# Two groups of FFN tiles ahead of the first down projection, and one more group with the gate in block products

## The chip, the cores and the metric

The kernel runs on one core of one Trainium2 chip. The metric is device time in microseconds (us) of one execution; the time before is the median of three runs, 1040.7 us (1040.25 to 1043.4).

## The reference

Two decoder layers on a sequence of 512 tokens with 1024 channels, in float32. Each layer is a normalized mixer with a residual, then a normalized gated FFN with a residual; at the end comes one more normalization. The FFN is what the change touches:

```
g  = hn @ w_gate                   # 1024 -> 2816
g  = causal_dwconv3(g, conv_w) + conv_b
up = hn @ w_up                     # 1024 -> 2816
h  = h + (silu(g) * up) @ w_down   # 2816 -> 1024
```

## The kernel before

**Number format.** Every matrix product is done in three matmuls of a rounded 32-bit type (`mm3`, lines 132 to 135): each operand is split into a rounded high part and the remainder (`hi`, `lo`), and `hi*hi`, `hi*lo` and `lo*hi` are added in one PSUM bank. The splits cost work on the other engines: ScalarE (ACT) makes `hi`, VectorE (DVE) subtracts it from the original to get `lo` (`parts`, L128 and L129; `split`, L247 and L249). In `summed` (L120 to L122) ACT writes the negative of `hi` into `lo`, and an accumulating DMA issued by GpSimd (POOL) adds the original.

**Buffers.** Original weights land in `raw` (4 buffers, loaded by the queue of SyncE, SP); their halves lie in `whi` and `wlo` (6 each). PSUM has seven banks for products (`mm`) and one for small work (`aux`).

**The FFN.** Its 2816 channels are 22 tiles of 128, taken two at a time: a group is named by its first tile, f = 0, 2, ... 20. `hidden(f)` computes the two activation tiles of a group, `a_f` and `a_f+1`, in one of four ways:
- f = 0, `direct` with `normed` false: the input is `h` times its gain, not yet divided by its norm; the norm is applied when the products leave PSUM. In the same call stand `pair_weights(2, ...)`, which loads and splits the weights of group 2, and `normalize` (L566 on), four times, which rewrites the eight pairs `hg` with the normalized input and builds the sums `t23`, `t41` that the block products need. Only then comes `rest()`, which takes group 0 out of PSUM (L555, conv at L504 and L506, silu at L512, the product with POOL at L558, the product with `up` at L561, then the split into `a_hi`, `a_lo`).
- f = 2, `direct` with `normed` true: 96 matmuls of 128x512, first the two gate tiles (48), then the two up tiles.
- f = 6, 10, 14, 18, `both`: gate and up each as a 2x2 block product (two tiles of output channels, two halves of the input channels, two halves of the tokens) in seven products instead of eight, in the manner of Strassen. Each product is 12 matmuls of 128x256. The stationary sides are sums and differences of weight blocks (`s12`, `s34`, L652 to L659), which DVE builds and then splits.
- the others (4, 8, 12, 16, 20), `seven`: the up tiles as such a block product (84 matmuls of 128x256), the gate tiles directly (48 of 128x512).

**The order of the work.** `PARTS` (L474) cuts the tiles into parts. For each part the groups of that part are computed in turn, and then the part's tiles are multiplied with their rows of `w_down` and added: to `h` in layer 0 (`project`, L292), to `y`, tokens in partitions, in layer 1 (`group8`, add at L1009). The parts are (0, 2), (2, 6), (6, 10), (10, 14), (14, 18), (18, 22): the first down projection uses two tiles (48 matmuls of 128x512), the others four (96). In layer 0 the last part also transposes the parameters of layer 1 (`params`, L92). A scheduler orders the instructions at build time by priorities close to the program's order and its own estimates; each engine then runs its list strictly in order. Activation tiles `a` have four buffers for each half, block sums (`sum`) three, the rows that the convolution reads three.

Of the kernel before, what the change touches and what calls it, by code (L numbers as in the profile page):

```python
# [30 lines left out]
def tile_trunk(ctx: ExitStack, tc: tile.TileContext, x, norm_mix, norm_ffn, final_norm,  # L31
# [13 lines left out]
    def mm_bank(name):  # L45
        return ps_mm.tile([P, 512], F32, tag="mm", name=name)
# [22 lines left out]
    def params1():  # L69
        return params("1", [  # L70
            ("mix", rows_of(norm_mix[1]), NK), ("bsp", b_spatial[0], NK),
            ("ffn", rows_of(norm_ffn[1]), NK), ("cf", conv_rows(conv_ffn[1]), 3 * NF),
            ("bf", rows_of(b_conv_ffn[1]), NF)])
# [39 lines left out]
    def weights(src, a, b, name):  # L113
        return parts(*fetch(src, a, b, name))
# [108 lines left out]
    def newton(ms, n, name, r):  # L223


        sd = work("sd", n, name)
        nc.scalar.activation(sd, ms, AF.Sqrt)
        nc.vector.reciprocal(r, sd)
        nc.vector.tensor_tensor(ms, ms, r, ALU.mult)
        nc.vector.scalar_tensor_tensor(ms, ms, -0.5, r, op0=ALU.mult, op1=ALU.mult)  # L230
# [42 lines left out]
    def project(name, w, acts, ks, norm, before=None):  # L273

        for gi in range(2):
            c0 = gi * 512
            chunks = {}
            for i in range(0, len(ks), 2):
                k0 = min(ks[i], ks[i + 1])
                hi, lo = weights(  # L280
                    w[k0 * P : (k0 + 2) * P, c0 : c0 + 512].rearrange("(k p) c -> p k c", p=P),
                    2, 512, f"{name}_{gi}_{k0}")
                chunks[k0], chunks[k0 + 1] = (hi, lo, 0), (hi, lo, 1)

            def lhs(k, j):
                hi, lo, n = chunks[k]
                cs = slice(j * P, (j + 1) * P)
                return hi[:, n, cs], lo[:, n, cs]

            def done(j, ps):  # L290
                k = gi * 4 + j
                nc.vector.tensor_tensor(h[k], ps, h[k], ALU.add)  # L292
                if norm is not None:
                    norm.add(k)

            group(f"{name}{gi}", range(4), ks, lhs, lambda k, j: acts[k], 4, done,
                  before if gi == 0 else None)
# [173 lines left out]
            return nxt  # L471


    PARTS = ((0, 2), (2, 6), (6, 10), (10, 14), (14, 18), (18, 22))  # L474
    HALF = S // 2
    BOTH = (6, 10, 14, 18)
    NP = NK // 2
    PAIRS = [k for i in range(NP) for k in (i, i + NP)]

# [7 lines left out]
    class Ffn:  # L487
# [307 lines left out]
        def hidden(self, f, before=lambda i, j: None):  # L795
            if f == 0:
                def first(i, j):
                    before(i, j)
                    if (i, j) == (1, 0):
                        self.norm.rstd_tokens()  # L800
                    elif (i, j) == (2, 2):
                        self.r = self.norm.rstd_spread()

                ch = self.pair_weights(0, [("g", 0), ("u", 0), ("g", 1), ("u", 1)])
                rest = self.direct(0, False, (range(4),), ch, first)
                self.ch = self.pair_weights(2, [("g", 0), ("g", 1), ("u", 0), ("u", 1)], "g")
                for kp in range(NP):
                    self.normalize(kp)
                rest()
            elif f == 2:  # L810
                self.direct(2, True, ((0, 1), (2, 3)), self.ch)()
            elif f in BOTH:
                self.both(f)
            else:
                self.seven(f)

    def ffn0(norm):
        nonlocal prm1
        with tc.tile_pool(name="f0", bufs=1) as ap:
            def sums(kp):  # L820
                return [ap.tile([P, 2, HALF], F32R, name=f"t23{i}_{kp}") for i in "hl"]

            ffn = Ffn(0, prm0, norm, ap, sums)
            nxt = None
            for a, b in PARTS:
                for f in range(a, b, 2):
                    ffn.hidden(f)
                if b == NF:
                    prm1 = params1()
                    nxt = Norm("m1", lambda k: prm1("mix", k))  # L830
                project(f"d0_{a}", w_ffn_down[0], ffn.acts, list(range(a, b)), nxt)
            return nxt
# [126 lines left out]
    def ffn1(norm):  # L959
        with tc.tile_pool(name="f1", bufs=1) as ap:  # L960
            def sums(kp):
                return [cp.tile([P, 2, HALF], F32R, tag=f"h{k}", name=f"t23_{k}")
                        for k in (kp, kp + NP)]

            ffn = Ffn(1, prm1, norm, ap, sums)
            acts = ffn.acts
            y = [ap.tile([P, D], F32, name=f"y{t}") for t in range(NT)]
            ssf = ap.tile([P, NT, PAD], F32, name="ssf")[:, :, :2]

            def turn_residual(t, half):  # L970
                ps = mm_bank(f"hT{t}_{half}")
                for i in range(4):
                    nc.tensor.transpose(ps[:, i * P : (i + 1) * P],
                                        h[half * 4 + i][:, t * P : (t + 1) * P], ident)
                nc.scalar.copy(y[t][:, half * 512 : (half + 1) * 512], ps)

            def before(i, j):
                if i < 2:
                    turn_residual(j, i)

            for a, b in PARTS:
                for f in range(a, b, 2):
                    ffn.hidden(f, before=before)
                last = b == NF
                if last:
                    fin = wp.tile([P, D], F32, tag="raw", bufs=4, name="fin")
                    nc.scalar.dma_start(
                        fin, final_norm.rearrange("(o d) -> o d", o=1).to_broadcast([P, D]))
                    root = small[:, 2:3]
                    nc.scalar.activation(root, eps, AF.Sqrt)  # L990
                ch = {}
                for ft in range(a, b):
                    ch[ft] = weights(w_ffn_down[1][ft * P : (ft + 1) * P, :]
                                     .rearrange("(k p) c -> p k c", p=P), 1, D, f"dn1_{ft}")

                def lhs(ft, j):
                    ts_ = slice((j // 2) * P, (j // 2 + 1) * P)
                    return acts[ft][0][:, ts_], acts[ft][1][:, ts_]

                def rhs(ft, j):  # L1000
                    c = slice((j % 2) * 512, (j % 2 + 1) * 512)
                    return ch[ft][0][:, 0, c], ch[ft][1][:, 0, c]

                yf = {}

                def done(j, ps):
                    t, half = j // 2, j % 2
                    dst = y[t][:, half * 512 : (half + 1) * 512]
                    nc.vector.tensor_tensor(dst, ps, dst, ALU.add)  # L1009
                    if not last:  # L1010
                        return
                    sq = tp.tile([P, S], F32, tag="sq", name=f"sqf{j}")
                    ss = ssf[:, t, half : half + 1]
                    nc.scalar.activation(sq, dst, AF.Square, accum_out=ss)
                    yf[half] = ap.tile([P, S], F32, tag="s", bufs=3, name=f"yf{j}")
                    nc.vector.tensor_tensor(yf[half], dst, fin[:, half * 512 : (half + 1) * 512],
                                            ALU.mult)
                    if half == 0:
                        nc.vector.tensor_scalar(ss, ss, 1.0 / D, EPS, op0=ALU.mult, op1=ALU.add)
                        return  # L1020
                    ms = ssf[:, t, 0:1]
                    nc.vector.scalar_tensor_tensor(ms, ss, 1.0 / D, ms, op0=ALU.mult, op1=ALU.add)
                    r = tp.tile([P, LINE], F32, tag="rc", name=f"rc_fin{t}")[:, :1]
                    newton(ms, 1, f"fin{t}", r)
                    nc.vector.tensor_scalar(ms, ms, 1.5, None, op0=ALU.add)
                    for c in range(2):
                        cs = slice(c * 512, (c + 1) * 512)
                        nc.vector.tensor_scalar(y[t][:, cs], yf[c], r, ms,
                                                op0=ALU.mult, op1=ALU.mult)
                        nc.sync.dma_start(out[t * P : (t + 1) * P, cs], y[t][:, cs])  # L1030

                group8(f"dn{a}", list(range(a, b)), lhs, rhs, 4, done)
# [12 lines left out]

    n = mixer0()
    n = ffn0(n)
    n = mixer1(n)
    ffn1(n)


# [28 lines left out]
```

## Time and profile before

| | |
|---|---|
| runs (3) | 1040.25, 1040.7, 1043.4 us; median 1040.7 |
| profiled execution | 1041.7 us, its span 1040.0 us |
| mean granted clock of TensorE | 0.983 |
| DVE busy | 660.4 us, 64% of the span |
| HBM read, written | 98.42 MB, 2.10 MB |

In the profile PE is TensorE's matmuls and PEld its weight loads, which run beside them. A row of the timeline gives start and duration in us, the engine, the line, the operation, the tiles (output <- inputs), and in brackets how long the engine had been idle and what released it. A row of the waits gives the engine and what it wanted, what it waited for, the total in us, the count and the longest. `d` are the banks of the down projection in layer 0, `dn` in layer 1, `gu` those of groups 0 and 2, `u_4a` and the like those of a block product of group 4. A matmul's duration contains the filling and draining of the array, so successive matmuls overlap, and the pace is read from starts.

### The profile page before, as it was taken

To read this page: it belongs to the slowest core of one execution; us is meant where nothing else is said; L and a number is where in the kernel's file an instruction comes from. 1 tells how busy PE (TensorE), PEld (TensorE's weight loads), DVE (VectorE), ACT (ScalarE), POOL (GpSimd) and SP (SyncE) were. 2 spreads that over 40 slices of the span, in tenths; PEclk is the share of its full clock that TensorE was granted. 3 is DMA by queue.
4 is the path that set the end of the run, shared out by engine and by line. 5 is a ranking of instruction groups with operands and counts; after the bars stand their busy time and mean duration, and the time that the engine had idled before them with its cause. 6 is when DMAs were issued, how large, how long until landed. Compare 5 with 4: busy or idle time off the path is not lost.

```text
span 1040.0 us, 13829 instructions
## 1 busy us (share of the span) xinstructions
PE 999.5 (96%) x5475; PEld 865.6 (83%) x5475; DVE 660.4 (64%) x977; ACT 495.0 (48%) x725; POOL 91.9 (9%) x107
## 2 busy tenths in 40 slices
PE   8999996899999999999999999949999999999997
PEld 6888885688988989899888888837889899898985
DVE  5976539638576586756833545495477756767576
ACT  6423447235453536436655434662426436353463
POOL 3041121100000000000300001220000000000000
PEclk9999998799999999999999999979999999999999
DMA  7432244324354453554343223451335544354432
GB/s 234 166 102 81 83 120 110 94 77 123 104 142 112 133 138 106 142 135 124 119 130 101 81 86 97 101 117 45 89 94 142 142 124 141 82 142 142 123 82 81
DMA packets 80462, 119.25 MB, mean 115 GB/s; under 512 B 4133, under 2 KB 53517, under 8 KB 80397
## 3 DMA queue, kind: packets, MB, share of 16 engines
q1 hardware_dynamic: 73580, 98.96, 30.2%
q0 software_dynamic: 5472, 17.83, 9.7%
q10 hardware_dynamic: 1344, 1.58, 0.5%
q8 instruction: 43, 0.70, 0.3%
q14 instruction: 23, 0.18, 0.1%
HBM read 98.42 MB, written 2.10 MB: 97 GB/s over the span
## 4 chain that ended last, share of the span: by engine, by line
PE 91%; DVE 3%; issue 3%; DMA 2%; ACT 0%; SPq 0%; POOL 0%; DVEq 0%; POOLq 0%; ACTq 0%
PE d L133 4%; PE d L134 4%; PE dn L135 4%; PE dn L133 4%; PE dn L134 4%; PE d L135 4%; PE g L133 4%; PE g L134 4%; PE g L135 3%; PE gu L133 2%; PE gu L135 2%; PE gu L134 2%; PE v L133 1%; PE oo L135 1%; PE u L134 1%
## 5 line engine op out<-in xcount | busy, mean ns | idle before, releaser
L133 PE MATMUL dn<-whi_dn,a_hi 128*128 128x512 f32 x176 | 69.3, 395 | 14.9 <-ACT a_hi L247 14.9
L133 PE MATMUL d<-a_hi,whi_d 128*128 128x512 f32 x176 | 68.1, 398 | 14.6 <-ACT a_hi L247 14.6
L134 PE MATMUL d<-a_lo,whi_d 128*128 128x512 f32 x176 | 69.4, 396 | 0.0
L134 PE MATMUL dn<-wlo_dn,a_hi 128*128 128x512 f32 x176 | 68.9, 393 | 0.0
L135 PE MATMUL d<-a_hi,wlo_d 128*128 128x512 f32 x176 | 68.9, 392 | 0.0
L135 PE MATMUL dn<-whi_dn,a_lo 128*128 128x512 f32 x176 | 68.5, 394 | 0.0
L506 DVE SCALAR_TENSOR_TENSOR c<-rows,prm,c 128x512 f32<-128x512 f32 x88 | 66.5, 770 | 0.4
L133 PE MATMUL g<-hgh,whi_g 128*128 128x512 f32 x160 | 62.5, 391 | 0.0
L134 PE MATMUL g<-hgl,whi_g 128*128 128x512 f32 x160 | 62.5, 391 | 0.0
L135 PE MATMUL g<-hgh,wlo_g 128*128 128x512 f32 x160 | 62.2, 389 | 0.0
L1009 DVE TENSOR_TENSOR y<-dn,y 128x512 f32<-128x512 f32 x48 | 32.8, 690 | 37.1 <-PE dn L135 37.0
L133 PEld LDWEIGHTS dn<-whi_dn,a_hi 128*128 128x128 f32 x176 | 33.4, 190 | 22.7 <-ACT a_hi L247 16.0
L133 PEld LDWEIGHTS d<-a_hi,whi_d 128*128 128x128 f32 x176 | 33.3, 191 | 22.6 <-ACT a_hi L247 15.9
L129 DVE TENSOR_TENSOR wlo_dn<-raw_dn,whi_dn 128x1024 fp32r<-128x1024 f32 x22 | 26.8, 1224 | 35.4 <-ACT whi_dn L128 35.4
L129 DVE TENSOR_TENSOR wlo_d<-raw_d,whi_d 128x1024 fp32r<-128x1024 f32 x22 | 26.8, 1224 | 35.4 <-ACT whi_d L128 35.4
L129 DVE TENSOR_TENSOR wlo_g<-raw_g,whi_g 128x1024 fp32r<-128x1024 f32 x24 | 29.3, 1222 | 30.4 <-ACT whi_g L128 26.6
L292 DVE TENSOR_TENSOR h<-d,h 128x512 f32<-128x512 f32 x48 | 32.7, 689 | 20.1 <-PE d L135 19.5
L247 ACT ACTIVATE a_hi<-s 128x512 fp32r<-128x512 f32 x44 | 27.4, 628 | 34.3 <-DVE s L792 13.3
L121 POOL DMA_DIRECT2D wlo_u<-raw_u x18 | 15.4, 858 | 306.6 <-ACT wlo_u L120 175.6
L129 DVE TENSOR_TENSOR wlo_u<-raw_u,whi_u 128x1024 fp32r<-128x1024 f32 x16 | 19.6, 1224 | 34.2 <-ACT whi_u L128 34.1
L135 PEld LDWEIGHTS dn<-whi_dn,a_lo 128*128 128x128 f32 x176 | 33.3, 189 | 8.5 <-DVE a_lo L249 1.3
L134 PEld LDWEIGHTS d<-a_lo,whi_d 128*128 128x128 f32 x176 | 33.6, 191 | 7.9 <-DVE a_lo L249 0.7
(911 smaller groups left out, 3135.7 us busy)
## 6 DMA issues: line engine op xcount, KB each, us to landing
raw_u<-in_w_ffn_up_dram SPq DMA_DIRECT2D x36, 512.0 KB, 3.8
raw_g<-in_w_ffn_gate_dram SPq DMA_DIRECT2D x36, 512.0 KB, 4.5
raw_d<-in_w_ffn_down_dram SPq DMA_DIRECT2D x22, 512.0 KB, 3.6
raw_dn<-in_w_ffn_down_dram SPq DMA_DIRECT2D x22, 512.0 KB, 3.7
wlo_u<-raw_u POOLq DMA_DIRECT2D x18, 512.0 KB, 5.2
wlo_g<-raw_g POOLq DMA_DIRECT2D x12, 512.0 KB, 5.1
raw_oe<-in_w_out_even_dram SPq DMA_DIRECT2D x8, 512.0 KB, 3.5
raw_g<-in_w_ffn_gate_dram SPq DMA_DIRECT2D x16, 256.0 KB, 2.8
```

The source lines that it names most:

```text
L121: nc.gpsimd.dma_start(lo, raw, accum_op=ALU.add)
L129: nc.vector.tensor_tensor(lo, raw, hi.bitcast(F32), ALU.subtract)
L133: nc.tensor.matmul(ps, lhs[0], rhs[0], start=start, stop=False)
L134: nc.tensor.matmul(ps, lhs[0], rhs[1], start=False, stop=False)
L135: nc.tensor.matmul(ps, lhs[1], rhs[0], start=False, stop=stop)
L247: nc.scalar.activation(hi, src, AF.Copy, scale=scale)
L292: nc.vector.tensor_tensor(h[k], ps, h[k], ALU.add)
L506: nc.vector.scalar_tensor_tensor(c, t[:, i : S + i], prm("cf", i * NF + ft), c, op0=ALU.mult, op1=ALU.add)
L1009: nc.vector.tensor_tensor(dst, ps, dst, ALU.add)
```

## The change

Two edits in the FFN, both for both layers. The list of parts now names the groups to be computed ahead of each projection: groups 0 and 2 come before the projection of tiles 0 and 1, and group 4 alone before that of tiles 2 to 5. And group 4 goes from `seven` to `both`, so that five of the nine block groups have the gate in block products too.

```
-    PARTS = ((0, 2), (2, 6), (6, 10), (10, 14), (14, 18), (18, 22))
+
+    PARTS = (((0, 2), 0, 2), ((4,), 2, 6), ((6, 8), 6, 10), ((10, 12), 10, 14),
+             ((14, 16), 14, 18), ((18, 20), 18, 22))
     HALF = S // 2
-    BOTH = (6, 10, 14, 18)
...
-            elif f in BOTH:
+            elif f % 4 == 2 or f == 4:
                 self.both(f)
...
-            for a, b in PARTS:
-                for f in range(a, b, 2):
+            for groups, a, b in PARTS:
+                for f in groups:
                     ffn.hidden(f)
...
-            for a, b in PARTS:
-                for f in range(a, b, 2):
+            for groups, a, b in PARTS:
+                for f in groups:
                     ffn.hidden(f, before=before)
```

In the order that the scheduler builds, PE's list has the 96 matmuls of group 2 ahead of the 48 of the small projection in both layers, 168 matmuls of 128x256 for group 4 in place of 84 and 48, and the parameter transposition of layer 0 behind group 20 instead of behind group 0. POOL has one accumulating DMA more per layer. SP issues the same loads; only the four of group 4 change places among themselves. All lines of the kernel after L474 move down by one.

## Prediction

> **What bounds the kernel now.** I read the page's busy shares first, then what TensorE (PE) waited for, then its timeline around the longest waits.
>
> ```profile
> PE 999.5 (96%) x5475; PEld 865.6 (83%) x5475; DVE 660.4 (64%) x977; ACT 495.0 (48%) x725; POOL 91.9 (9%) x107
> PE   8999996899999999999999999949999999999997
> PEclk9999998799999999999999999979999999999999
> ```
>
> PE carries the span, with two dips (slices 7 and 8, and 27; the clock falls in the same slices). The waits say what they are:
>
> ```profile
> PE dn L133 <- ACT a_hi L247: 14.9, 2, 14.3
> PE d L133 <- ACT a_hi L247: 14.6, 2, 14.2
> ```
>
> In each layer PE waits once for some 14 us at the first matmul of the small down projection, for `a_hi`, the activations of FFN tile 0. PE's timeline, layer 0 and then layer 1:
>
> ```profile
> 172.02 0.40 PE L135 MATMUL gu<-hgh,wlo_u 128*128 128x512 f32 x1
> 172.25 0.26 PE L92 MATMUL prm_ps<-ident,pk 112*128 112x112 f32 x1
> 186.71 1.22 PE L133 MATMUL d<-a_hi,whi_d 128*128 128x512 f32 x2 [14.20 <-ACT a_hi L247]
> ...
> 201.10 0.39 PE L133 MATMUL gu<-hgh,whi_g 128*128 128x512 f32 x1
> ...
> 222.86 0.28 PE L623 MATMUL u_4a<-hgh,whi_a 128*128 128x256 f32 x1
> ...
> 243.86 0.40 PE L133 MATMUL d<-a_hi,whi_d 128*128 128x512 f32 x1
> ...
> 265.68 0.28 PE L623 MATMUL g_6a<-hgh,whi_a 128*128 128x256 f32 x1
> ...
> 285.83 0.28 PE L623 MATMUL u_8a<-hgh,whi_a 128*128 128x256 f32 x1
> ...
> 686.70 0.39 PE L135 MATMUL gu<-hgh,wlo_u 128*128 128x512 f32 x1
> 701.38 0.80 PE L133 MATMUL dn<-whi_dn,a_hi 128*128 128x512 f32 x1 [14.30 <-ACT a_hi L247]
> ...
> 715.23 0.39 PE L133 MATMUL gu<-hgh,whi_g 128*128 128x512 f32 x1
> ...
> 736.99 0.28 PE L623 MATMUL u_4a<-hgh,whi_a 128*128 128x256 f32 x1
> ...
> 757.98 0.40 PE L133 MATMUL dn<-whi_dn,a_hi 128*128 128x512 f32 x1
> ```
>
> So in layer 0: group 0 ends at 172.25, the small projection runs from 186.71, group 2 from 201.10, group 4 from 222.86, the next projection from 243.86. Durations overlap on PE, so all prices below are differences of starts. The stretches around the wait also show the clock:
>
> ```profile
> 180.00:190.00 10.00, 3.29 (x7) 1.99 (x7) 10.00 (x12) 4.78 (x7) 4.67 (x4) 0.50 0.67 157
> 190.00:192.00 2.00, 1.56 (x4) 0.96 (x4) 1.52 (x4) 0.63 (x1) 0.00 (x0) 0.50 0.00 0
> 192.00:203.00 11.00, 11.00 (x49) 9.06 (x48) 6.82 (x10) 1.69 (x2) 0.00 (x0) 0.97 0.15 48
> ```
>
> (Columns: sum, PE, weight loads, DVE, ACT, POOL busy; then granted clock, DMA.) When PE comes back at 186.71 its clock is 0.50 and stays there until about 192. The hole thus costs its 14 us and a slow start behind it. DVE is full from 180 to 190: it normalizes `h`, and evacuates group 0 in the same queue.
>
> **The change, part by part.**
>
> *1. Group 2 ahead of the small projection.* It does not wait for `a_0`, only for the normalized `hg`. Its 96 matmuls took 222.86 - 201.10 = 21.76 us, 0.227 each. The 48 of the projection cost 48 x 0.227 = 10.88 at that pace; they took 201.10 - 186.71 = 14.39 in layer 0 and 13.85 in layer 1, the rest being the slow clock and a second wait of about 0.5. New start of group 2: 172.25. Is its input there? PE needs the pairs of `hg` in order, each pair of k feeding 12 matmuls (2.72 us) of the first set: at 172.25, 174.97, 177.7 and 180.4. The last halves come from DVE:
>
> ```profile
> 176.36 0.69 DVE L555 TENSOR_TENSOR rows<-gu,rstd_f 128x512 f32<-128x512 f32 x1
> 176.96 1.30 DVE L576 TENSOR_TENSOR hgl<-x,hgh 128x512 fp32r<-128x512 f32 x2
> ...
> 185.32 0.68 DVE L561 TENSOR_TENSOR s<-gu,s 128x512 f32<-128x512 f32 x1
> ...
> 190.84 0.68 DVE L249 TENSOR_TENSOR a_lo<-s,a_hi 128x512 fp32r<-128x512 f32 x1
> ...
> 691.63 1.29 DVE L576 TENSOR_TENSOR hgl<-x,hgh 128x512 fp32r<-128x512 f32 x2
> ```
>
> They are done at 178.26 (layer 1: 692.92, wanted at 686.93 + 8.16 = 695.1), about 2 us early. Weights of group 2 were loaded and split before in both orders (SP's list keeps its order here, but for group 4's four loads). Banks: group 0 holds four of seven until DVE reads them; the first set of group 2 takes two, the second the seventh and the one that `rows<-gu` has read at 177.05. No wait, price 0.
>
> *2. What follows on ACT and DVE.* Before, ACT waited for DVE ahead of each `a_hi`:
>
> ```profile
> 186.03 0.63 ACT L247 ACTIVATE a_hi<-s 128x512 fp32r<-128x512 f32 x1 [2.57 <-DVE s L561]
> ...
> 190.17 0.63 ACT L247 ACTIVATE a_hi<-s 128x512 fp32r<-128x512 f32 x1 [2.76 <-DVE s L561]
> ```
>
> ```profile
> L504 ACT ACTIVATE c<-rows,prm 128x512 f32<-128x512 f32 x44 | 31.7, 720 | 0.4
> ```
>
> In the built order ACT now has, ahead of `a_0_hi`, the two `whi_a` of group 4, two copies `rows<-gu_2` and one tap `c_2`; ahead of `a_1_hi` also `c_3` and `s_2`. Copies wait for PE's first set, done at 172.25 + 10.88 = 183.13, when ACT comes to them at about the same time, so nobody behind them (`a_0_hi`, whose input comes at 185.3 + 0.68) is held. On DVE three taps of group 2 and two `wlo_a` come ahead of `a_1_lo`, in place of four sums of group 4 and a parameter copy. ACT: seven instructions of at most 0.72 (a tap, the dearest of them), 5.0 us more, against 2.57 + 2.76 = 5.3 that it waited there. Between the product at 185.32 and `a_1_lo` DVE has three taps and a `wlo_a` (3 x 0.77 + 0.69 = 3.0) for three sums and the copy (3 x 0.69 + 0.26 = 2.3), 0.7 more; I allow 0.5 for the two `whi_a`, which ACT has ahead of `s_0`. So `a_1_lo` ends at 191.52 + 1.2 = 192.7. PE wants it when it has done group 2 and three matmuls: 172.25 + 21.76 + 0.68 = 194.7. Margin 2 us; without it each us late costs one, plus the slow clock once the wait is as long as above.
>
> *3. Group 4 in block products for gate and up.* It takes away 84 matmuls of 128x256 with 48 of 128x512 (243.86 - 222.86 = 21.00) and puts 168 of 128x256, as group 6 has them: 285.83 - 265.68 = 20.15. Gain 0.85. Its price lies elsewhere: seven stationary sets instead of six, and only 10.88 us of projection before it starts, instead of 10.88 + 21.76. I put the work in DVE's queue from `a_1_lo` on:
>
> ```profile
> L652 DVE TENSOR_TENSOR s12g<-raw_g,raw_g x8: 684/688/694, 246.9 to 950.5; 128x512 f32<-128x512 f32 x8
> ```
>
> ```profile
> L633 DVE TENSOR_TENSOR wlo_s12g<-s12g,whi_s12g 128x1024 fp32r<-128x1024 f32 x8 | 9.8, 1222 | 0.0
> L292 DVE TENSOR_TENSOR h<-d,h 128x512 f32<-128x512 f32 x48 | 32.7, 689 | 20.1 <-PE d L135 19.5
> L506 DVE SCALAR_TENSOR_TENSOR c<-rows,prm,c 128x512 f32<-128x512 f32 x88 | 66.5, 770 | 0.4
> L632 ACT ACTIVATE whi_s12g<-s12g 128x1024 fp32r<-128x1024 f32 x8 | 8.5, 1063 | 14.7 <-DVE s12g L653 14.7
> L121 POOL DMA_DIRECT2D wlo_u<-raw_u x18 | 15.4, 858 | 306.6 <-ACT wlo_u L120 175.6
> wlo_u<-raw_u POOLq DMA_DIRECT2D x18, 512.0 KB, 5.2
> ```
>
> Until `wlo_s12u` is done: one tap (0.77), seven sums, two gates times `s`, two `a_lo` and six adds to `h` (17 x 0.69), three `wlo` (3 x 1.22): 16.2 us, 192.7 + 16.2 = 208.9. PE starts group 4 at 172.25 + 21.76 + 10.88 = 204.89; its products take 20.15 / 14 = 1.44, and the fifth, `u` 5, is the first to want `s12u`, at 210.6. Margin 1.7 with full durations, more because DVE's steps overlap (176.96 follows 176.36, 0.60 after the start of a step of 0.69). The DMA half of `up`: its ACT steps end near 208 (the weight buffer comes free with the projection, 204.9, then about 1 us each), POOL 0.9, landing 5.2: 214.1; wanted by the ninth product at 216.4. Banks: the eighth output of the projection wants the first one's bank back at 194.0 + 7 x 1.36 = 203.5, the add behind `a_3_lo` reads it near 202. I take 0; as the upper end I keep a wait as long as both margins, 1.7 + 2.3 = 4.0 us per layer. Below 0 it cannot be: PE's work is counted without any wait.
>
> *4. The projection after group 4.* Now a group with two gates in block products ends right ahead of it, so `a_4` comes later after the last product. In the built order 23 matmuls on `a_2`, `a_3` (5.2 us) stand ahead of the first on `a_4`, 15 before. From the last product: an add to `kept`, a tap, two products, a shared `wlo_a`, `a_4_hi` and `a_4_lo`, some 5.5 us with `s_4` between. Price 0 to 1 per layer; I take 0. POOL gains one accumulating DMA per layer (0.86 and 5.2 to land); it had 28.66 us of idle time ahead of the next:
>
> ```profile
> 255.72 0.86 POOL L121 DMA_DIRECT2D wlo_g<-raw_g  x1 [28.66 <-DVE h L292]
> ```
>
> ```profile
> 496.41 1.22 DVE L129 TENSOR_TENSOR wlo_v<-raw_v,whi_v 128x1024 fp32r<-128x1024 f32 x1
> ```
>
> *5. The parameter transposition* (0.26) leaves the hole of layer 0 and goes ahead of the last projection of layer 0, whose first wait then has 10 matmuls of cover instead of 17. Bounds 0.26 and 0.26 + 7 x 0.227 = 1.85; in the built order the split `wlo_v` at 496.41 (1.22) no longer stands before the last product of `s_20`, so I take 0.26.
>
> **Sum.** Layer 0, from the end of group 0 to the start of the second projection: 243.86 - 172.25 = 71.61 before; 21.76 + 10.88 + 20.15 = 52.79 after; 18.82 gained. Layer 1: 757.98 - (686.70 + 0.23) = 71.05 against 52.79; 18.26. Together 37.08, less 0.26: 36.8. The profiled execution took 1041.7 (its span of 1040.0 and 1.7 around it), hence 1004.9; it stands 1.0 above the median of 1040.7, so the median goes to **1003.9**.
>
> *A rule that speaks against part 3.* Measured on this chip, the smaller matmul is dear per column only a little: 0.120 (1.44 / 12) for 256 columns, 0.227 for 512. The Trainium skill, "TensorE: Matmul & The Clock Gate", section "Back-to-back issue gap", says that in a stream of load and matmul pairs the spacing is set by both, about 81 ns for 128 columns and 131 ns for 512. By a line between these, an estimate of about 98 ns for 256, group 4 would take 16.5 instead of 14.5 us, 2.0 longer where I count 0.85 shorter, 5.7 us of gain less in both layers. The rows of this trace differ from it (0.227 against 0.131), and the measurement decides.
>
> **Rivals.**
> - *A. Late stationary sets.* ACT, DVE or POOL fall behind by more than my margins, and PE waits in group 4 or at `a_1`, `a_4`. For: DVE is full from 171 on, and the room ahead of group 4 falls from 32.6 to 10.9 us. Against: DVE's sums above fit. Price 2 to 8 us per layer with the slow clock: 1008 to 1020, say 1012.
> - *B. The hole moves.* PE reaches group 2 but waits for the last normalized pair before it goes on, as it did for `a_0`. 178.26 - 172.25 = 6.0, and 3.5 of slow start (14.39 - 10.88), per layer: 1003.9 + 19 = 1022.9. For: DVE writes that pair last. Against: 36 matmuls do not need it.
> - *C. Block products paced by weight loads.* If each of the 168 waited for its own load (0.19, as 33.4 us for 176 in the rows of `dn`), group 4 would take 31.9 us, 11.8 more per layer: 1027.5. Against: group 6 shows 20.15. The rule of the Trainium skill above is a milder form of it.
> - *D. Slower.* The preparation of group 4 starts only when the projection is over, and its engines work one after the other: DVE two `wlo_a`, eight sums, four `wlo` (11.8), ACT two halves and eight full passes (9.7), together 21.5, with 3.5 of slow start: 25.0 against 18.5 gained, 6.5 lost per layer, 1053.7. It decides from a wait of 18.5 on. Against: in the built order the first five sums stand ahead of the projection's adds, and none reads its result.
>
> ```profile
> L133 PEld LDWEIGHTS dn<-whi_dn,a_hi 128*128 128x128 f32 x176 | 33.4, 190 | 22.7 <-ACT a_hi L247 16.0
> ```
>
> **How the numbers follow.** Forecast (the holes closed, at most 3 us of new waits) 0.80; A 0.13; B 0.03; C 0.01; D 0.02; no effect 0.01, if PE's list were not what it is. A measurement of this kernel can tell about 0.3%, 3.1 us, from no change. Faster: forecast, A, B, C, 0.97; same 0.01; slower 0.02. The range begins at 1002.5, the sum without its 0.26, the 0.45 between the median and the fastest run, and some 0.7 for nine starts read to 0.1. It ends at 1012, which is the price named for A and what parts 3 and 5 give at their upper ends (2 x 4.0): left out are half of A, B, C, D and no effect, 0.14.
>
> **What would show it.** Right: the two waits on `a_hi` of 14 us are gone from PE's list, the dips in those slices are filled, the clock row is 9 throughout; PE starts group 2 some 21.8, the small projection 10.9 and group 4 20.2 us before what follows. Wrong: a PE wait on `hgl` in group 2 (B), on `wlo_s12u`, `wlo_u` or a bank in group 4 (A), products of more than 1.44 us (C), or DVE idle behind a wait for PE in front of group 4's sums (D).

## The result and the profile after

The changed kernel took **1005.1 us** (median of 4 runs, 1004.69 to 1006.14), the kernel before 1041.3 (4 runs, 1040.25 to 1043.4): a ratio of 0.9651, 95% interval 0.9633 to 0.9669. The forecast was 1003.9, the range 1002.5 to 1012. The profiled execution took 1006.1, the slowest of the four, with a span of 1004.4.

The page after, busy shares and the two rows of slices that had the dips:

```profile
PE 992.1 (99%) x5547; PEld 865.9 (86%) x5547; DVE 666.0 (66%) x993; ACT 499.9 (50%) x735; POOL 94.1 (9%) x109
...
PE   8999999999999999999999999999999999999997
...
PEclk9999999999999999999999999999999999999999
```

Slices 7, 8 and 27 are full and the clock row is 9 throughout. PE's waits after (total, times, longest); between these two rows the list has two more, of 1.3 and 1.1 us:

```profile
PE wst L851 <- POOL ws L844: 1.6, 1, 1.6
...
PE z L134 <- DVE hgl L370: 1.0, 2, 0.8
```

Both waits on `a_hi`, 29.5 us together, are gone. Three of the four rows lie in the first 40 us and were there before. The first, a wait for the spatial weights that PE transposes (`wst`), is new, and lies in the second mixer, which the change does not touch; experiments 1 and 5 look at it. PE's timeline, the first instruction of each stage, layer 0 and then layer 1:

```profile
171.78 0.39 PE L133 MATMUL gu<-hgh,whi_g 128*128 128x512 f32 x1
...
193.53 0.39 PE L133 MATMUL d<-a_hi,whi_d 128*128 128x512 f32 x1
...
204.41 0.28 PE L624 MATMUL g_4a<-hgh,whi_a 128*128 128x256 f32 x1
...
224.57 0.40 PE L133 MATMUL d<-a_hi,whi_d 128*128 128x512 f32 x1
...
691.37 0.39 PE L133 MATMUL dn<-whi_dn,a_hi 128*128 128x512 f32 x1
...
722.41 0.40 PE L133 MATMUL dn<-whi_dn,a_hi 128*128 128x512 f32 x1
```

Read as differences: group 2 takes 193.53 - 171.78 = 21.75 us, the small projection 10.88, group 4 20.16; in layer 1 the last two together take 31.04 as well. From the end of group 0 to the second projection layer 0 takes 52.79 us in place of 71.61. That is the 18.82 of the forecast to the hundredth. In layer 1 the second projection and the group behind it give 18.28 (group 6 starts 35.59 earlier than before, 744.23 against 779.82; the first transposition of that layer, `hT`, started 17.31 earlier, 641.99 against 659.30).

### The profile page after: what moved, and what is told of

The parts are those of the page before. It is cut to its first block, busy times and chain, and to the rows that moved or that the text cites. A ratio compares the mean times of both kernels' runs of the same rounds, so it can differ in the third digit from the quotient of the medians.

```text
span 1004.4 us, 14019 instructions
## 1 busy us (share of the span) xinstructions
PE 992.1 (99%) x5547; PEld 865.9 (86%) x5547; DVE 666.0 (66%) x993; ACT 499.9 (50%) x735; POOL 94.1 (9%) x109
## 4 chain that ended last, share of the span: by engine, by line
PE 95%; DMA 2%; DVE 2%; ACT 1%; SPq 0%; issue 0%; POOL 0%; DVEq 0%; ACTq 0%; POOLq 0%
PE dn L133 4%; PE dn L135 4%; PE dn L134 4%; PE d L133 4%; PE d L134 4%; PE d L135 4%; PE gu L133 3%; PE g L133 3%; PE g L134 3%; PE gu L134 3%; PE gu L135 3%; PE g L135 3%; PE u L135 1%; PE oo L133 1%; PE oo L135 1%; PE u L134 1%
## 5 line engine op out<-in xcount | busy, mean ns | idle before, releaser
L507 DVE SCALAR_TENSOR_TENSOR c<-rows,prm,c 128x512 f32<-128x512 f32 x88 | 68.9, 792 | 0.3
L133 PE MATMUL g<-hgh,whi_g 128*128 128x512 f32 x128 | 50.0, 391 | 0.0
L134 PE MATMUL g<-hgl,whi_g 128*128 128x512 f32 x128 | 50.0, 391 | 0.0
L135 PE MATMUL g<-hgh,wlo_g 128*128 128x512 f32 x128 | 49.8, 389 | 0.0
L120 ACT ACTIVATE wlo_g<-raw_g 128x1024 fp32r<-128x1024 f32 x14 | 14.7, 1050 | 51.6 <-PE dn L134 51.6
L513 ACT ACTIVATE s<-c,prm 128x512 f32<-128x512 f32 x44 | 31.6, 718 | 16.7 <-DVE c L507 16.6
L135 PEld LDWEIGHTS d<-a_hi,wlo_d 128*128 128x128 f32 x176 | 33.0, 188 | 6.8
```

What stands on the lines that cost most here:

```text
L120: nc.scalar.activation(lo, raw, AF.Copy, scale=-1.0)
L133: nc.tensor.matmul(ps, lhs[0], rhs[0], start=start, stop=False)
L134: nc.tensor.matmul(ps, lhs[0], rhs[1], start=False, stop=False)
L135: nc.tensor.matmul(ps, lhs[1], rhs[0], start=False, stop=stop)
L507: nc.vector.scalar_tensor_tensor(c, t[:, i : S + i], prm("cf", i * NF + ft), c, op0=ALU.mult, op1=ALU.add)
L513: nc.scalar.activation(s, c, AF.Silu, bias=self.prm("bf", ft))
```

## The experiments

Ten kernels ran, in three sets, each set beside runs of the kernel before on the same chip (medians 1042.4, 1041.7 and 1041.8 there). Nothing is left out of the computation in any of them; three do needless work besides.

**1. The order alone.** Group 4 as it was, seven block products and a gate.

```diff
-            elif f % 4 == 2 or f == 4:
+            elif f % 4 == 2:
```

> Only the order of the change: groups 0 and 2 ahead of the small projection, group 4 in its old form (seven block products and a 512-wide gate). Theory (the order closes the hole, group 4's block products give 0.85 us per layer, and 1.6 us are lost to a new wait for the transposed spatial weights, wst): the time of the changed kernel and 2 x 0.85 more, 1005.1 + 1.7 = 1006.8, with the wst wait in it. Rival 1 (the block products give nothing, or their preparation eats what they give): 1005.1 or less. Rival 2 (the wst wait is chance of one execution): the wait is absent here, 1005.2.

Measured: 1007.1 us (1006.9 to 1008.6), ratio 0.9666 [0.9649, 0.9682]. Its timeline in layer 0:

```profile
194.07 0.39 PE L133 MATMUL d<-a_hi,whi_d 128*128 128x512 f32 x1
...
204.95 0.28 PE L624 MATMUL u_4a<-hgh,whi_a 128*128 128x256 f32 x1
...
225.94 0.40 PE L133 MATMUL d<-a_hi,whi_d 128*128 128x512 f32 x1
```

Group 4 takes 20.99 us, 0.83 more than in block products, and the two layers together 1.7. The order alone therefore gives about 35 us (1042.4 - 1007.1) of the 37. The wait on `wst` was 0.2 here, with the same program in that place: so theory and rival 2 were each half right, the time as the theory had it, the wait as the rival had it.

**2. The block products alone**, in the old order.

```diff
-    PARTS = (((0, 2), 0, 2), ((4,), 2, 6), ((6, 8), 6, 10), ((10, 12), 10, 14),
+    PARTS = (((0,), 0, 2), ((2, 4), 2, 6), ((6, 8), 6, 10), ((10, 12), 10, 14),
```

> Only group 4 in fourteen block products, the order of the work as before. Theory: each layer's group 4 takes 20.15 us instead of 21.0, the two 14 us waits for a_hi stay: 1041.3 - 1.7 = 1039.6. Rival 1 (products paced by their weight loads): group 4 longer than 21 us, 1045 or more. Rival 2 (its seven stationary sets disturb the queue that group 0's evacuation shares with them, in the hole): the wait for a_hi grows by as much as the products save, 1041.3 or more.

Measured: 1038.5 us (1037.2 to 1039.2), ratio 0.9960 [0.9946, 0.9975], so 3.9 less than the kernel before (2.6 to 5.6 by the interval), where 1.7 was expected. Layer 0:

```profile
172.74 0.26 PE L92 MATMUL prm_ps<-ident,pk 112*128 112x112 f32 x1
...
186.17 0.80 PE L133 MATMUL d<-a_hi,whi_d 128*128 128x512 f32 x1 [13.17 <-ACT a_hi L247]
...
222.14 0.28 PE L624 MATMUL g_4a<-hgh,whi_a 128*128 128x256 f32 x1
...
242.29 0.40 PE L133 MATMUL d<-a_hi,whi_d 128*128 128x512 f32 x1
```

Group 4 takes 20.15: the 0.85 are there, as the theory had them. The rest is the hole, 13.43 us from the end of group 0 in place of 14.46. The timeline of DVE and POOL, first of the kernel before, then of this one, shows why:

```profile
182.93 1.91 POOL L558 TENSOR_TENSOR s<-s,rstd_f 128x512 f32<-128x512 f32 x1 [1.49 <-ACT s L512]
183.02 0.70 DVE L729 TENSOR_TENSOR s<-raw_u,raw_u 128x512 f32<-128x512 f32 x1
183.63 1.77 DVE L506 SCALAR_TENSOR_TENSOR c<-rows,prm,c 128x512 f32<-128x512 f32 x1
```

```profile
183.41 1.31 POOL L559 TENSOR_TENSOR s<-s,rstd_f 128x512 f32<-128x512 f32 x1 [1.49 <-ACT s L513]
184.76 0.69 DVE L562 TENSOR_TENSOR s<-gu,s 128x512 f32<-128x512 f32 x1 [0.97 <-POOL s L559]
185.37 0.74 DVE L507 SCALAR_TENSOR_TENSOR c<-rows,prm,c 128x512 f32<-128x512 f32 x1
```

Before, a sum of group 4 and a tap (a step of the convolution) stand ahead of the product `s` that `a_0` is made of (its row, 185.32, is in the prediction). Here the sum is not there and the tap comes behind, and `s` starts 0.56 us sooner though group 0 ended 0.49 later (172.74 against 172.25). The durations say where the 1.05 us come from. Before, POOL's product, which this `s` reads, took 1.91 us beside the sum, and the tap took 1.77 us beside POOL; here, with neither of the two steps there, POOL's product takes 1.31, and the same tap, once it comes, 0.74. So the product is done 11.98 us after the end of group 0 in place of 12.59, and `s` follows it after 0.04 us in place of 0.48. The last section comes back to the two engines. The expectation, that the hole would be the same or longer, was wrong. In the changed kernel this second gain is worth nothing, as there is no hole for it to shorten.

**3. What the hole costs: needless matmuls in it.** The kernel before, with 48 and with 64 matmuls of the first normalized tile ahead of the small projection.

```diff
+    def filler(layer):
+        ps = mm_bank(f"fill{layer}")
+        for i in range(48):
+            nc.tensor.matmul(ps, hg[0][0][:, :P], hg[0][0], start=i == 0, stop=i == 47)
...
+                if a == 0:
+                    filler(0)
```

> The kernel before with 48 needless matmuls (128x512, of the first normalized tile, result unused) between group 0 and the small projection: about 10.9 us of the 14 us hole are filled with work, the order of everything else stays. The wait for a_0 ends when it did (DVE and ACT do not hang on it), but PE comes to it at full clock. Theory 1 (the 3.5 us that the projection takes beyond its 10.88 are the slow clock): 3.0 to 3.5 less per layer, 1034.5 to 1035.5. Theory 2 (they are mostly a_1, which comes at 190.8, 4.1 us behind the projection's start, and which a projection at full clock would just wait for longer; 41 matmuls of 0.227 behind it end at about 200.1 instead of 201.1): 1.0 less per layer, 1039.3.

> The kernel before with 64 needless matmuls ahead of the small projection in place of 48, 14.5 us, so that nothing is left of the wait for a_0. With 48 a wait of 3.3 us stayed, the clock still fell to 0.50 some 1 to 1.5 us after PE came back, for about 3 us, and the projection took 12.6 in place of 14.4 us. Theory 1 (the whole loss behind the hole is the clock): no wait, no fall, the projection takes 10.9; group 2 starts 1.7 us earlier per layer than with 48, 1039.5 - 3.4 = 1036. Theory 2 (a_1, which comes 4.1 us behind a_0, takes its place: nine matmuls of 0.227 on a_0, then a wait of 2.0 us, then 39 matmuls, 12.9 in all, and a fall of the clock behind that wait): no less than with 48, 1039 to 1041.

Measured: with 48, 1039.5 us (1038.4 to 1040.6), ratio 0.9976 [0.9965, 0.9988]; with 64, 1040.4 (1040.2 to 1042.3), ratio 0.9991 [0.9982, 1.0001]. PE and its clock in the kernel with 64, in stretches (columns as in the prediction: sum, PE, weight loads, DVE, ACT, POOL busy, then granted clock and DMA):

```profile
186.00:188.00 2.00, 1.49 (x7) 0.81 (x5) 2.00 (x4) 1.35 (x2) 0.23 (x1) 1.00 0.95 329
188.00:190.00 2.00, 1.81 (x8) 1.42 (x8) 2.00 (x3) 0.00 (x0) 1.28 (x1) 1.00 0.01 3
190.00:191.00 1.00, 0.31 (x2) 0.00 (x0) 1.00 (x2) 0.53 (x1) 0.00 (x0) 1.00 0.00 0
```

and its timeline there:

```profile
187.00 0.49 PE L133 MATMUL d<-a_hi,whi_d 128*128 128x512 f32 x1
188.19 0.50 PE L134 MATMUL d<-a_lo,whi_d 128*128 128x512 f32 x1 [0.70 <-DVE a_lo L249]
...
191.15 0.97 PE L133 MATMUL d<-a_hi,whi_d 128*128 128x512 f32 x3 [0.84 <-ACT a_hi L247]
...
200.16 0.39 PE L133 MATMUL gu<-hgh,whi_g 128*128 128x512 f32 x1
```

The clock is 1.00 from end to end, and the small projection still takes 200.16 - 187.00 = 13.16 us, where at its pace it needs 10.88 (13.17 in layer 1). The 14.39 of the kernel before are thus not mainly the slow clock. A projection at full clock reaches `a_lo` of tile 0 and then tile 1 too soon, and waits for them (0.70 and 0.84 in the rows above; by starts each costs about 1.0 us: 1.19 and 1.23 to the next matmul in place of 0.23). At half clock it came to them later, and the wait for tile 1 was 0.44 long. What the slow clock cost is about the difference, 14.39 - 13.16 = 1.23 us in layer 0 and 13.85 - 13.17 = 0.68 in layer 1. Theory 2 holds, but for the fall of the clock that it expected behind the wait, and theory 1 falls. With 48 the projection took 12.61, also because its list of matmuls there has more of tile 0 first; the order of a list that the scheduler writes is not the same from kernel to kernel, so the two fillers differ in more than their number.

**4. Normalizing later.** The changed kernel, with the last pair of tiles normalized five times.

```diff
-            for i, k in enumerate((kp, kp + NP)):
-                nc.vector.scalar_tensor_tensor(x[:, i, :], h[k], self.prm("ffn", k), r,
-                                               op0=ALU.mult, op1=ALU.mult)
+            for again in range(5 if kp == NP - 1 else 1):
+                for i, k in enumerate((kp, kp + NP)):
+                    nc.vector.scalar_tensor_tensor(x[:, i, :], h[k], self.prm("ffn", k), r,
+                                                   op0=ALU.mult, op1=ALU.mult)
```

> The changed kernel with the last pair of tiles normalized five times in place of once (eight needless DVE steps of 0.67 us, the same result), so that hgl comes 5.4 us later to group 2, where it had about 3 us to spare (done at 177.2, wanted at 180.2). It asks what each microsecond costs behind the margin. By DVE's order PE waits some 1.7 to 2.3 us in group 2 of each layer. Theory 1 (each microsecond late costs one, and so short a wait costs no clock): 3.4 to 5 more, 1008.5 to 1010. Theory 2 (the clock falls as after the 3.3 us that were left in the filled hole, where it stood at 0.50 for about 3 us): 1.5 more per layer, 1011.5 to 1013. Theory 3 (the margin was larger than read): 1005 to 1006.

Measured: 1015.7 us (1013.8 to 1017.5), ratio 0.9749 [0.9734, 0.9764], more than any of the three theories had. Its waits:

```profile
PE u_4b L625 <- DMA wlo_u<-raw_u: 3.8, 2, 2.0
PE u_4e L625 <- ACT whi_s12u L634: 1.6, 2, 1.0
```

No wait on `hgl` stands in its list. The scheduler laid PE's list out anew: matmuls of `up` with the first pairs now stand ahead of the gate's last ones, so group 2 lost only some 0.4 us. The price appears two stages on: the stationary sets of group 4 come late, and the projection and group 4 take 4.15 us longer in layer 0 and 4.26 in layer 1 with those 0.4. In layer 0:

```profile
195.02 0.39 PE L133 MATMUL d<-a_hi,whi_d 128*128 128x512 f32 x1
...
206.52 0.28 PE L625 MATMUL g_4a<-hgh,whi_a 128*128 128x256 f32 x1
...
229.77 0.40 PE L133 MATMUL d<-a_hi,whi_d 128*128 128x512 f32 x1
```

The projection takes 11.50 in place of 10.88 and group 4 23.25 in place of 20.16. That makes the 8.4 by which its span (1012.1) is longer than that of the changed kernel in experiment 5 (1003.7). The profiled execution was the fastest of its runs; what the others lost beyond it is not seen. The run was meant as a test of the margin in group 2 and doesn't serve as one; it is a test of rival A, whose mechanism it shows and whose price it puts at 4 us per layer for 5.4 us of DVE, in a list of PE that is not quite that of the changed kernel.

**5. The wait on `wst`.** The changed kernel again, unchanged; and with the transposition of the spatial weights two chunks later in its projection:

```diff
-            for q in range(2):
+            def turn_ws(k):
+                if k not in (4, 5):
+                    return
+                q = k - 4
                 ps = aux_bank(f"wst{q}")
...
-            in_group("v0", w, 1024, False, v_done(0), 2)
+            in_group("v0", w, 1024, False, v_done(0), 2, before=turn_ws)
```

> The changed kernel once more, unchanged, with more runs of it and of the kernel before on one chip. The profiled execution of the changed kernel (1006.14) was the slowest of its four and had a wait of 1.6 us on wst. Theory (that wait is chance: the load of the spatial weights reaches its first reader with no slack, and its landing varies from one execution to the next): median 1005.1 +- 0.6, a wst wait of another length, 0 to 1.6. Rival (it is there each time): the same wait of 1.6. For the base: if the profiled execution of before (1041.7) was an ordinary one and its first median of 1040.7 low, the median of before comes out at 1041.5 to 1042.5 and the gain at 36.5 to 37; if the first median was right, 1040.7 and 35.6.

> The changed kernel with the eight transpositions of the spatial weights (wst) put later in the first projection of the second mixer, two chunks of k (24 to 30 matmuls, 5.4 us) behind their old place, all else as it was. Theory (the miss of 1.2 us is the new wait of 1.6 us on wst): the wait is gone and nothing takes its place, 1005.1 - 1.6 = 1003.5. Rival (what comes behind is as late, as the first Gelu of v waits for the same bank, or PE waits at the next step): 1005 or more.

Measured: unchanged, 1004.9 us (1004.6 to 1005.4), before 1041.7 on the same chip, ratio 0.9647 [0.9633, 0.9660]; later, 1005.3 (1004.5 to 1005.4), before 1042.4, ratio 0.9642 [0.9628, 0.9656]. The unchanged kernel's wait was 0.3 in this execution, and here is what PE waited for, POOL's masking of the weights, and DVE's step beside it. First the execution profiled first (PE waits 1.55), then this one (0.32):

```profile
505.25 1.23 DVE L129 TENSOR_TENSOR wlo_v<-raw_v,whi_v 128x1024 fp32r<-128x1024 f32 x1 [0.94 <-ACT whi_v L128]
505.42 2.01 POOL L844 TENSOR_SCALAR_AFFINE_SELECT ws<-ws 128x1024 f32<-128x1024 f32 x1 [2.79 <-DMA ws<-in_w_spatial_dram]
...
507.48 0.66 PE L851 MATMUL wst<-ident,ws 128*128 128x128 f32 x4 [1.55 <-POOL ws L844]
```

```profile
505.44 1.09 POOL L845 TENSOR_SCALAR_AFFINE_SELECT ws<-ws 128x1024 f32<-128x1024 f32 x1 [2.48 <-DMA ws<-in_w_spatial_dram]
505.59 2.02 DVE L130 TENSOR_TENSOR wlo_v<-raw_v,whi_v 128x1024 fp32r<-128x1024 f32 x1 [0.94 <-ACT whi_v L129]
...
506.60 0.66 PE L852 MATMUL wst<-ident,ws 128*128 128x128 f32 x4 [0.32 <-POOL ws L845]
```

Two steps of one program, 0.15 us apart either way round: the one that starts first takes its usual time, the other about 0.8 to 0.9 longer, and PE waits for POOL's. So the theory of chance holds for most of the wait: it is a race between a load's landing and the step of ACT ahead of DVE's. The later transposition takes the wait away (that span was 1002.8, and the row is gone), but its ratio is not told apart from the unchanged kernel's. That the miss of the forecast lies in this wait is not borne out: the unchanged kernel, with only 0.3 us of it in its profiled execution, has nearly the same median (1004.9 against 1005.1). What the executions without a profile waited there is not seen.

**6. More block products.** All groups from 4 on, and the same with the later transposition; then groups 8 to 20 in layer 0 alone.

```diff
-            elif f % 4 == 2 or f == 4:
+            elif f >= 4:                                             # all
+            elif f % 4 == 2 or f == 4 or f > 4 and self.layer == 0:  # layer 0
```

> The changed kernel with groups 8, 12, 16 and 20 also in fourteen block products, so that all nine groups from 4 on have that form. Theory (each group saves 0.85 us per layer, and DVE and ACT have room for the additional sums and halves: DVE is busy 66%, ACT 50%): 8 x 0.85 = 6.8 less, 1005.1 - 6.8 = 998.3. Rival 1 (the sets of two such groups in a row come late, since no gate group with its cheaper preparation lies between): waits on wlo_s12u or wlo_u in groups 6, 10, 14, 18, time at or above 1005. Rival 2 (products paced by their weight loads): groups of more than 21 us, above 1007.

> Both together: all nine groups in block products, and the transposition of the spatial weights later in its projection. Theory: what the all-products kernel gives (998.3) less the wst wait, which was 0 to 1.6 us in the profiled executions so far, hence 0 to 1.6 less: 997.0 to 998.3. Rival: the later transposition costs what it saves, no difference.

> The changed kernel with groups 8, 12, 16 and 20 in fourteen block products in layer 0 alone. In the profile of the kernel with all nine groups in that form, layer 0 from its second projection to the next mixer took 271.4 us in place of 273.9, and layer 1 to its last projection 256.4 in place of 252.6, where DVE's sums for the next group wait for their load and hold the reading of the banks behind them. Theory (layer 0 keeps its gain, layer 1 is as it was): 2.5 less, 1005.0 - 2.5 = 1002.5. Rival (the gain of layer 0 was chance, or its groups disturb what follows): 1004.5 to 1006.

Measured: all 1005.9 us (1004.6 to 1008.3), ratio 0.9652 [0.9639, 0.9666]; with the later transposition 1005.0 (1004.8 to 1006.1), 0.9649 [0.9636, 0.9662], where about 998 was expected of both; layer 0 alone **1002.5** (1002.2 to 1003.0), ratio 0.9624 [0.9609, 0.9638]. PE's waits with all:

```profile
PE g_18e L624 <- DVE rows L692: 2.7, 2, 2.4
...
PE g_6e L624 <- DVE rows L692: 0.7, 1, 0.7
```

Rival 1 of the expectation had the time (1005 or above) and the groups, but not the tile: PE waits for no stationary set. The waits lie in the groups *ahead of* the changed ones, on the reading of their banks. SP's and DVE's timelines in layer 1 say why, for group 6 with group 8 behind it:

```profile
746.53 0.37 SPq L110 DMA_DIRECT2D raw_g<-in_w_ffn_gate_dram  x1
```

```profile
751.26 0.69 DVE L653 TENSOR_TENSOR s12g<-raw_g,raw_g 128x512 f32<-128x512 f32 x1 [2.70 <-DMA raw_g<-in_w_ffn_gate_dram]
...
757.77 0.69 DVE L653 TENSOR_TENSOR s12u<-raw_u,raw_u 128x512 f32<-128x512 f32 x1 [1.34 <-DMA raw_u<-in_w_ffn_up_dram]
...
758.98 0.42 DVE L692 TENSOR_TENSOR rows<-g_6e,rows 128x256 f32<-128x256 f32 x1
```

The sums of a group in block products need both halves of a weight, four loads into four buffers, and the second half of `gate` is not issued until 746.5. DVE stands at the first sum for 2.70 us, then makes six more steps of preparation, and only then, at 756.01, reads a first bank of group 6. It stands again for 1.34 us at the first sum of `up`, whose second half was issued at 753.90, and the reading of `g_6e`, for which PE waits, comes at 758.98. In layer 1 groups 6, 10 and 18 take 21.2, 22.1 and 24.4 us in place of 20.3; in layer 0 only group 18 is late (20.7), and from its second projection to the next mixer that layer takes 271.4 us in place of 273.9. Hence the version with layer 0 alone, which comes out 2.5 us lower, as expected, and is the fastest of all, 39.3 us below the kernel before on its chip (the two kernels ran on different chips, and their intervals still overlap: it reaches up to 0.9638, the changed kernel's down to 0.9633).

## Why the prediction was nearly right, and where not

- *Group 2 closes the hole:* right, 21.75 + 10.88 + 20.16 against the 21.76 + 10.88 + 20.15 of the sum.
- *The margins of group 2 and group 4:* none was used up, and all were wider than given. Rows of DVE, POOL and PE after, from their timeline:

```profile
176.50 1.28 DVE L577 TENSOR_TENSOR hgl<-x,hgh 128x512 fp32r<-128x512 f32 x2
...
204.78 1.23 DVE L634 TENSOR_TENSOR wlo_s12u<-s12u,whi_s12u 128x1024 fp32r<-128x1024 f32 x1
...
206.94 0.86 POOL L121 DMA_DIRECT2D wlo_u<-raw_u  x1 [8.14 <-ACT rows L682]
...
229.00 0.63 ACT L247 ACTIVATE a_hi<-s 128x512 fp32r<-128x512 f32 x1 [0.51 <-DVE s L707]
...
229.81 0.84 PE L133 MATMUL d<-a_hi,whi_d 128*128 128x512 f32 x3
```

  The half of the last pair that group 2 wants first was done about 177.2 (the row holds two) and wanted at 180.16; `a_1_lo` ended at 191.65, where 192.7 was forecast; `wlo_s12u` at 206.0, forecast 208.9, and PE came to it at 210.4; the DMA half of `up` landed at 211.5 (206.94 + 4.6), forecast 214.1, wanted at 216.2. DVE's steps follow each other 0.60 after a start where I counted 0.69 each.
- *The projection after group 4, price 0:* right, but with nothing to spare: `a_4_hi` ended at 229.63, and the 24th matmul of that projection, by the built order the first that reads it, began at 229.81.
- *Block products in group 4, 0.85 per layer:* right (0.83 in layer 0 between experiment 1 and the changed kernel).
- *The parameter transposition, 0.26:* about 0.1 in place of it (from the transposition at 476.52 to the next mixer's `v` at 498.51 the last projection of layer 0 takes 21.99 us, before 517.62 - 495.76 = 21.86).
- *"The hole thus costs its 14 us and a slow start behind it", and the 14.39 us of the projection, "the rest being the slow clock and a second wait of about 0.5":* the sum is right, the division is not. Experiment 3 shows that without any fall of the clock the projection still takes 13.16 us, held by `a_lo` of tile 0 and by tile 1; the clock is about 1.2 of the 3.5 us. The prices of rivals B and D, which count 3.5 us of slow start, rest on this and would have been too high.
- *The last step of the sum, "it stands 1.0 above the median of 1040.7, so the median goes to 1003.9":* **this is where 1.0 of the 1.2 us of the miss come from.** The gain of 36.8 made against the profiled execution gives 1004.9. The profiled execution of before (1041.7) was an ordinary one: with more runs the medians of the kernel before are 1041.3, 1042.4, 1041.7 and 1041.8, and on one chip with the changed kernel again the gain is 1041.65 - 1004.94 = 36.7. The first median, of three runs spread over 3.2 us, was low by about 1, and I took its error over into the forecast. Between the two profiled executions the gain is only 1041.7 - 1006.1 = 35.6; there the 1.55 us of `wst` are missing, a wait for which the sum had no term.
- *The rivals:* A did not occur, though experiment 4 shows its mechanism when DVE is 5 us later, and experiment 6 a relative of it when one more group asks for its sets: DVE, held by a load, reads the banks late. B, C and D did not: no wait in group 2, products of 1.44, and DVE's sums ahead of the projection's adds. The milder form of C, after the Trainium skill ("TensorE: Matmul & The Clock Gate", "Back-to-back issue gap"), gave by estimate 16.5 us for group 4 in its new form against 14.5 in its old one, 2.0 longer. Measured, it took 20.16 against 20.99, 0.83 shorter, and no run here shows the rule's spacing.

The order's gain is shown by experiment 1, the block products' by 1 and 2. What the slower runs of experiment 4 lost beyond their profile is not settled.

## What to carry to other kernels

When an engine waits for something that another computes, look for a block of its own work that needs none of it and is as long as the wait, and move the whole block there; then price it by differences of starts, stage by stage, and look at what is prepared for the stage *behind*, where the lost time shows up when a margin is gone. Do not credit a slow clock after a hole before asking whether the next input would have been there for a faster engine. And make a sum against one execution: a median of three runs that spread over 3 us is no better base than that execution.

## What the runs showed of the hardware

The granted clock did not fall at once, nor after every wait. In the changed kernel PE waited 1.55 us (`wst`) and the clock stayed at 1.00 in each stretch up to 513; a wait of 1.97 in experiment 4 (`u_4b` in layer 1, ended at 721.47) left it at 1.00 too. With a wait of 3.3 us in the kernel with 48 needless matmuls it fell, after PE was back, to half:

```profile
186.00:188.00 2.00, 1.49 (x5) 1.21 (x6) 2.00 (x4) 1.18 (x2) 0.72 (x1) 0.76 0.74 256
188.00:190.00 2.00, 2.00 (x6) 1.61 (x5) 2.00 (x3) 0.03 (x1) 0.79 (x1) 0.50 0.00 0
190.00:192.00 2.00, 2.00 (x9) 1.59 (x8) 1.33 (x3) 0.60 (x1) 0.00 (x0) 0.89 0.00 0
```

(PE came back at 186.51.) With all groups in block products a wait of 2.35 us, ended at 951.10, did the same a little later:

```profile
952.00:953.00 1.00, 1.00 (x8) 1.00 (x7) 1.00 (x2) 0.00 (x0) 0.10 (x1) 0.65 0.45 86
953.00:954.00 1.00, 1.00 (x7) 1.00 (x6) 1.00 (x4) 0.12 (x1) 0.00 (x0) 0.50 1.07 205
```

But the same wait in the same place, with the later transposition beside, was 2.40 us long and left the clock at 1.00 in each stretch up to 960:

```profile
949.28 0.39 PE L624 MATMUL g_18e<-hgh,whi_s34g 128*128 128x256 f32 x1 [2.40 <-DVE rows L692]
```

So in these runs waits of up to 1.97 us left the clock alone, those of 3.3 us or more halved it, and about 2.4 us did once and once not: the length of the wait does not decide alone. In stretches of a quarter of a microsecond the fall begins 3.8 us after PE stopped in layer 0 of the kernel with 48, 2.9 us in its layer 1 (there half a microsecond before PE was back), and 3.6 us in the kernel with all groups, and it lasts 3.4 us in all three. What it cost shows in group 18: 24.4 us with the fall, 23.0 without.

The Trainium skill ("TensorE: Matmul & The Clock Gate", "Why this matters for your kernels") asks for no gaps of more than about 3 us on this engine. The row of 2.35 us shows the fall below that here, the row of 2.40 us shows none.

POOL and DVE held each other up. The two fences of experiment 5 show it from both sides, 2.01 against 1.09 us for the one and 2.02 against 1.23 for the other; those of experiment 2 show it in the hole, where POOL's product took 1.91 against 1.31 and DVE's tap 1.77 against 0.74. The Trainium skill ("SBUF — State Buffer", "SBUF: two separate sides") says that the two share a pair of ports which the one that starts first holds for its whole instruction, also for a DVE step with two inputs in this memory against a POOL step that reads it. The rows of experiment 5 agree: were the later step held until the earlier one ends, POOL would end at 505.25 + 1.23 + 1.09 = 507.57 and DVE, in the other execution, at 505.44 + 1.09 + 1.23 = 507.76; they ended at 507.43 and 507.61.
